# Projection in the order q, k, v, products moved from GpSimd to VectorE, and regrouped transposes in a one-core hybrid layer

## The chip, the cores and the metric

The kernel runs on one core of a Trainium2 chip. The core has a matrix engine (TensorE, PE in the profile; PEld are its weight loads), three engines for elementwise work (VectorE or DVE, ScalarE or ACT, GpSimd or POOL), and SyncE (SP), which issues most of the transfers that the 16 DMA engines carry out. The metric is the device time of one execution in microseconds (us), with smaller being better.

## The reference

One layer of an encoder on 512 tokens of width 1024, all in float32:

```python
h = rms_norm(x, norm1_g) * (1 + sc1) + sh1
z = h @ w_in
xr, xg, q, k, v, qi, ki, wi = jnp.split(z, ...)
y_rnn = rg_lru_branch(xr, xg, ...)
q = rms_norm(q.reshape(B, S, N_HEADS, HEAD_DIM), q_norm_g)
k = rms_norm(k.reshape(B, S, N_HEADS, HEAD_DIM), k_norm_g)
...
y_attn = dsa_attention(q, k, v, qi, ki, wi)
mix = jnp.concatenate([rms_norm(y_rnn, rg_out_g), rms_norm(y_attn, attn_out_g)], axis=-1) @ w_out
x = x + g1 * mix
h2 = rms_norm(x, norm2_g) * (1 + sc2) + sh2
ff = moe_ffn(h2.reshape(B * S, D), w_router, b_router, w1, b1, w2, b2).reshape(B, S, D)
return x + g2 * ff
```

The attention has 8 heads of 64; an indexer picks up to 128 keys for each query. In the last part every token goes to 4 of 32 experts; an expert multiplies its tokens by `w1` (1024 x 2048, 8 MB), applies a clamped gated unit, and multiplies by `w2` (1024 x 1024, 4 MB).

## The kernel before

The program is written in the order of the work, and a scheduler puts each engine's instructions in a fixed order: an instruction that is ready early by its estimate can pass others that stand before it in the source. Each engine then works through its own list, and waits where an operand isn't there.

**The head** (until about 400 us). The columns of z are made in pieces of 256 columns. `split_in` writes a piece of the weights as a rounded part (ScalarE, line 152) and a rest (line 153, on VectorE, or on GpSimd where the caller passes `G`, as for xr, xg and k); `mm3` (lines 157 to 159) adds three products of the parts. The order of the pieces is: v's second half with the indexer's keys, the indexer's queries, xr, xg, then k, v's first half, and q. `norm_heads` squares a head group on ScalarE (454), sums it on VectorE (455) and takes the inverse root in twelve small steps (`rstd_of`, lines 141 to 148). `prep_k` scales k on VectorE (462), transposes it on TensorE (468) and splits it (469, 470); `prep_q` does so for q (475 to 480) after a scaling of q's four tiles, which VectorE and GpSimd share (553). `rg_half` prepares the recurrent branch's half of the output product, and `split_out` the output weights: GpSimd multiplies them by the gate g1 (491), ScalarE and VectorE split them (492, 493). `rg_out_half` is one of eight products of that half; four stand before attention, four are given to `attend` as filling.

`attend` takes one tile of 128 queries through 8 heads: two products for the scores (576, 577), a masked minimum on VectorE (581), the exponential on ScalarE (582), transposes (587), a copy (588) and the products with the values (569). After the first `attend` the kernel splits the experts' first bias into three bf16 parts, on GpSimd (680 to 686). The output product's second half, the router and the norm of the second part follow.

**The experts** (from about 400 us to the end). SyncE loads all weights in order into 18 places of 1 MB (`wslot`, line 823): 8 for an expert's `w1`, 4 for its `w2`. A load waits until TensorE has read what lay in its place. The places lie in memory that the head uses until its end.

Experts are ranked by their number of tokens, and each rank has a number of 32-row blocks, `NBS`, 1 to 4 (86 in all). For expert j the loop issues: `gather` of expert j+2's rows from HBM (GpSimd, 855), `up(j)` (884), `glu(j)` (889 to 893), `turn_x(j+1)`, which transposes the gathered rows (863, copied by ScalarE and VectorE in turn, 864), `bias(j+1)` (870, 871), `down(j-1)` (911, 917), `add_out(j-1)`, which scales the result (930) and adds it to the output in HBM row by row (GpSimd, 933), and `turn_act(j)` (901, 902). `turn_x`, `bias`, `turn_act` and `route` take two PSUM banks in turn, 4 and 5; `up` writes banks 0 to 3, `down` banks 6 and 7. `up` and `down` use TensorE in tiles of 32 columns, the transposes use the whole array. `gather` and `add_out` move all of a rank's rows, 32 for each block, whether a slot holds a token or not. A loop at the end handles tokens beyond a rank's rows, in blocks of 128.

## Time and profile before

| | |
|---|---|
| median of 3 runs | 1457.71 us (1455.44 to 1466.08) |
| profiled execution | 1457.75 us |
| its span, first to last instruction | 1455.9 us |
| mean granted TensorE clock | 0.963 |
| busy: TensorE, VectorE, ScalarE, GpSimd | 1363.4, 547.6, 273.3, 204.1 us |
| DMA | 482.39 MB, mean 331 GB/s |

In the profile a line such as L491 is a line of the program. A row of a timeline gives start, duration, engine, line, operation, and in square brackets how long the engine had been idle and what released it. A row of the view by stretches gives each engine's busy time and instructions, the granted TensorE clock (1.00 is full speed), the mean busy share of the DMA engines, and GB/s. A row of the view by groups gives count, busy time, mean ns of one, idle time before, and its releasers.

### The profile page before, as it was taken

Reading aid. Unit: us, or ns where it says so; the run is one execution under the profiler, and the core shown is the slowest. Engines: PE = TensorE matmul, PEld = TensorE weight load, DVE = VectorE, ACT = ScalarE, POOL = GpSimd, SP = SyncE. Lnnn points to the kernel's source line nnn. Section 1 sums busy time; section 2 is a strip of 40 time slices with the busy share of each in tenths; the row PEclk is TensorE's granted clock in tenths of the full one; section 3 lists DMA queues with packets and bytes.
Section 4 is the critical chain, followed back from the end, with each engine's and each line's share of the span. In section 5 each row is a group of like instructions: output and inputs, shape, how many; then the busy total and the mean of one; then the engine's idle time right before and its main releaser. Section 6 shows DMA issues by size and latency. Waiting matters only on the chain. (4 is left out here: it accounts for less than half of the span.)

```text
span 1455.9 us, 26502 instructions
## 1 busy us (share of the span) xinstructions
PE 1363.4 (94%) x10907; PEld 611.4 (42%) x10907; DVE 547.6 (38%) x1317; ACT 273.3 (19%) x552; POOL 204.1 (14%) x238
## 2 busy tenths in 40 slices
PE   5999988999799999999999999999999999999993
PEld 2854887767533343334333333333333333333320
DVE  4579986755722222214212231223132122212221
ACT  4445553433111100101011000001010010100100
POOL 4312623511100010000001011000000000100000
PEclk9999999878689999999999999999999999999997
DMA  9676113014999999999999999999999999999995
GB/s 373 219 270 231 59 59 117 22 58 159 374 390 363 323 404 392 391 407 404 409 395 403 418 401 383 402 410 389 410 399 404 409 405 407 399 393 393 395 418 197
DMA packets 83398, 482.39 MB, mean 331 GB/s; under 512 B 11778, under 2 KB 14018, under 8 KB 33098
## 3 DMA queue, kind: packets, MB, share of 16 engines
q1 hardware_dynamic: 75034, 453.88, 77.8%
q0 software_dynamic: 7520, 24.68, 6.7%
q8 instruction: 87, 1.43, 0.4%
q10 hardware_dynamic: 720, 2.10, 0.4%
q14 instruction: 37, 0.30, 0.1%
HBM read 465.14 MB, written 15.48 MB: 330 GB/s over the span
## 5 line engine op out<-in xcount | busy, mean ns | idle before, releaser
L884 PE MATMUL bank<-mem,mem 128*32 128x512 f32 x5504 | 622.4, 595 | 0.0
L884 PEld LDWEIGHTS bank<-mem,mem 128*32 128x32 f32 x5504 | 174.6, 110 | 371.6 <-issue 363.2
L911 PE MATMUL bank<-mem,mem 128*32 128x512 f32 x2304 | 268.4, 593 | 0.0
L889 DVE TENSOR_TENSOR bank<-bank,mem 128x512 f32<-128x512 f32 x86 | 60.0, 697 | 410.1 <-PE bank L884 409.8
L911 PEld LDWEIGHTS bank<-mem,mem 128*32 128x32 f32 x2304 | 85.0, 110 | 146.0 <-issue 134.1
L891 ACT ACTIVATE mem<-bank 128x256 f32<-128x256 f32 x86 | 33.1, 385 | 527.8 <-DVE bank L889 527.8
L930 DVE SCALAR_TENSOR_TENSOR mem<-bank,gate_h,mem 64x512 f32<-64x512 f32 x72 | 54.0, 749 | 207.2 <-PE bank L911 206.5
L933 POOL DMA_INDIRECT out_dram<-mem,idx_all x32 | 47.0, 1470 | 581.7 <-DVE mem L930 525.9
L157 PE MATMUL bank<-mem,mem 128*128 128x512 f32 (+1 forms) x320 | 115.0, 362 | 2.9 <-DVE mem L522 2.3
L158 PE MATMUL bank<-mem,mem 128*128 128x512 f32 (+1 forms) x320 | 113.7, 355 | 0.0
L159 PE MATMUL bank<-mem,mem 128*128 128x512 f32 (+1 forms) x320 | 112.7, 352 | 0.0
L855 POOL DMA_INDIRECT mem<-h_d,idx_all x32 | 30.2, 943 | 400.4 <-PE bank L863 342.7
L157 PEld LDWEIGHTS bank<-mem,mem 128*128 128x128 f32 x320 | 62.3, 196 | 14.3 <-issue 3.5
L159 PEld LDWEIGHTS bank<-mem,mem 128*128 128x128 f32 x320 | 62.4, 195 | 12.9 <-issue 6.8
L917 PE MATMUL bank<-mem,mem 128*32 128x512 f32 x448 | 61.8, 601 | 6.0 <-SPq L1014 4.3
L158 PEld LDWEIGHTS bank<-mem,mem 128*128 128x128 f32 x320 | 62.6, 195 | 9.3 <-issue 3.5
L864 DVE COPY mem<-bank 128x512 f32<-128x512 f32 (+2 forms) x32 | 18.0, 564 | 112.5 <-PE bank L863 112.2
L863 PEld LDWEIGHTS bank<-ident,mem 128*128 128x128 f32 (+2 forms) x256 | 33.7, 196 | 58.7 <-issue 26.8
L902 ACT COPY mem<-bank 128x512 f32<-128x512 f32 (+1 forms) x32 | 18.3, 573 | 207.9 <-PE bank L911 115.3
L863 PE MATMUL bank<-ident,mem 128*128 128x128 f32 (+2 forms) x256 | 43.6, 295 | 11.2 <-ACT mem L902 5.1
L153 POOL TENSOR_TENSOR mem<-mem,mem 128x512 fp32r<-128x512 f32 (+1 forms) x28 | 41.2, 1490 | 86.4 <-ACT mem L152 86.3
L901 PEld LDWEIGHTS bank<-ident,mem 128*128 128x128 f32 x172 | 24.5, 207 | 37.5 <-issue 21.1
(325 smaller groups left out, 1216.9 us busy)
## 6 DMA issues: line engine op xcount, KB each, us to landing
mem<-in_w_dram SPq DMA_DIRECT2D x384, 1024.0 KB, 15.1
mem<-in_w_ada_dram SPq DMA_DIRECT2D x24, 1024.0 KB, 6.3
mem<-in_w_in_dram SPq DMA_DIRECT2D x20, 512.0 KB, 5.5
mem<-in_x_dram SPq DMA_DIRECT2D x8, 512.0 KB, 6.4
mem<-in_w_out_dram SPq DMA_DIRECT2D x8, 512.0 KB
mem<-in_w_in_dram SPq DMA_DIRECT2D x8, 256.0 KB, 5.9
mem<-mod_d SPq DMA_DIRECT2D x4, 512.0 KB, 6.0
h_d<-mem POOLq DMA_DIRECT2D x4, 512.0 KB, 8.6
```

The source lines that it names most:

```text
L153: (sub or V).tensor_sub(lo, src, hi)
L157: T.matmul(p, ah, bh, start=(k == 0), stop=False)
L158: T.matmul(p, al, bh, start=False, stop=False)
L159: T.matmul(p, ah, bl, start=False, stop=(k == n - 1))
L863: T.transpose(p[:, k, 0:n], xgs[frm][0:n, 4 * q + k::KD], ident[0:n, 0:n])
L884: T.matmul(bk[b][32 * n:32 * n + 32, :], xT[:, k, BT * b:BT * b + BT], w[k][:, 0, n * 512:(n + 1) * 512], start=(k == 0), stop=(k == KD - 1))
L889: V.tensor_add(bk[b], bk[b], biasb[j % 2])
L891: A.activation(act[:, b], u[:, :, 0], AF.Gelu_apprx_sigmoid)
L911: T.matmul(bk[6 + b // 2][o:o + 32, :], aT[:, b, c, BT * n:BT * n + BT], w[n][:, c, m * 512:(m + 1) * 512], start=(n + c == 0), stop=(n == ...
L917: T.matmul(bk[6 + nb // 2][o:o + 32, :], aT[:, nb - 1, c, BT * n:BT * n + BT], w[n][:, c, m * 512:(m + 1) * 512], start=(n == 0), stop=(n ...
L930: V.scalar_tensor_tensor(ys[64 * h:64 * h + a.stop - a.start, ns], p[a], gate_h[a, h, j:j + 1], g2h[a], op0=OP.mult, op1=OP.mult)
L933: G.indirect_dma_start(out=out_rows, out_offset=bass.IndirectOffsetOnAxis(ap=idx_all[a, j:j + 1], axis=0), in_=ys[a], in_offset=None, comp ...
```

## The change

- z's last pieces are made in the order q, k, v. q's load follows xr's weights, k's follows the rg inputs, v's comes last. q's norm, scaling and `prep_q` stand beside k's products; the weights of the recurrent half are split after k's second half, in the memory that k's weights leave; k's norm and `prep_k` stand beside and after v.
- The products with g1 in `split_out`, q's scaling and the bias split go from GpSimd to VectorE and ScalarE; the bias split is moved ahead of k's norm. The subtractions of line 153 for q and v go to GpSimd, where those for k are already.
- In the experts' loop `turn_x` stands after `down`, next to `turn_act`, and `add_out` after both. Its two copies are both on ScalarE. Where the current expert has fewer than four blocks, bank 3 is a third bank for `turn_x`, `bias` and `turn_act`.
- Each rank has a number of rows that is a multiple of 8 (2560 in all instead of 2752); `gather` and `add_out` move only those. The last 32 rows of the three gather buffers are cleared once.

```diff
     halves(ch_piece, w_xr, lambda a: (ev_xr, 2 * a), G)
-    w_k = load_in(R[0], 1536)
+    w_q = load_in(R[0], 1024)
     modulate(1)
     for b in range(4):
         rg_in(b)
+    w_k = load_in(R[1], 1536)
     halves(ch_piece, w_xg, lambda a: (ev_xg, 2 * a), G)
     rg_out()
-    w_v = load_in(R[1], 2048, 256)
+    w_v = load_in(R[2], 2048, 256)
...
-            G.tensor_mul(raw[b][:, 0], raw[b][:, 0], g1r)
+            V.tensor_mul(raw[b][:, 0], raw[b][:, 0], g1r)
...
-    halves(tok_piece, w_k, lambda a: (ev_tok(zk, 256 * a),), G)
-    rk = norm_heads(zk, "k", 191, rls)
-    tok_piece(w_v, ev_tok(zv, 0))
-    for pr in range(4):
-        prep_k(pr, rk)
-    w_q = load_in(R[2], 1024)
+    def split_b1():
+        for n in range(2):
...
+            V.tensor_scalar(b1o, b1o, 1.0, None, op0=OP.add)
+            A.copy(b1t[:, ns], b1f[0:96])
+            V.tensor_sub(b1f[0:96], b1f[0:96], b1t[:, ns])
+            for q in (1, 2):
+                c = slice(32 * q, 32 * q + 32)
+                A.copy(b1t[c, ns], b1f[c])
+            V.tensor_sub(b1f[64:96], b1f[64:96], b1t[64:96, ns])
+            A.copy(b1t[64:96, ns], b1f[64:96])
...
+    halves(tok_piece, w_q, lambda a: (ev_tok(zq, 256 * a),), G)
...
-    half_a = rg_half()
-    halves(tok_piece, w_q, lambda a: (ev_tok(zq, 256 * a),))
+    load_wo(0)
+    rq = norm_heads(zq, "q", 191.5, rls)
+    for i in range(NT):
+        z = zq[:, i].rearrange("p (h d) -> p h d", h=H)
+        V.tensor_mul(z, z, rq[:, i, :, None].to_broadcast([128, H, HD]))
+    k_half = lambda a: tok_piece(part_of(w_k, 256 * a, 256 * a + 256), ev_tok(zk, 256 * a), G)
+    k_half(0)
+    for pr in range(4):
+        prep_q(pr)
+    r_a = rg_half()
+    k_half(1)
+    half_a = (r_a, *split_out(0, R[1], grg))
+    split_b1()
+    rk = norm_heads(zk, "k", 191, rls)
+    tok_piece(w_v, ev_tok(zv, 0), G)
...
     load_wo(1)
+    for pr in range(4):
+        prep_k(pr, rk)
     rg = [partial(rg_out_half, i, n, *half_a) for i in (3, 2, 1, 0) for n in range(2)]
     for f in rg[0:4]:
         f()
-    rq = norm_heads(zq, "q", 191.5, [mem(174.75 + 2 * j, S) for j in range(2)])
-    for i in range(NT):
-        z = zq[:, i].rearrange("p (h d) -> p h d", h=H)
-        (G if i % 2 else V).tensor_mul(z, z, rq[:, i, :, None].to_broadcast([128, H, HD]))
-    for pr in range(4):
-        prep_q(pr)
...
+    ROWS = [96, 96, 128, 128, 128, 120, 112, 104] + [96] * 4 + [88] * 2 + [80] * 2 + [72] * 2 + [64] * 8 + [56] * 2 + [48] * 2 + [32] * 2
...
+    def spare(nb):
+        return bank(4, 5) if nb == 4 else bank(3, 4, 5)
...
-            (V.tensor_copy if q else A.copy)(xTs[j % 2][:, 4 * q:4 * q + 4, 0:n], p[:, :, 0:n])
+            A.copy(xTs[j % 2][:, 4 * q:4 * q + 4, 0:n], p[:, :, 0:n])
...
         if j + 1 < E:
-            turn_x(j + 1, xg_of(j + 1), NBS[j + 1])
-            bias(j + 1, bias_col(j + 1))
+            bias(j + 1, bias_col(j + 1), nb)
         if j:
             down(load_down(w2_of(expert(j - 1))), NBS[j - 1])
-            add_out(j - 1, NBS[j - 1])
+        if j + 1 < E:
+            turn_x(j + 1, xg_of(j + 1), NBS[j + 1], nb)
         if j < E:
             turn_act(nb)
+        if j:
+            add_out(j - 1, NBS[j - 1], ROWN[j - 1])
```

More of the change, by code (lines that the diff above doesn't have):

```diff
@@ L496, in layer @@
     ssA = const.tile([128, NT], F32)
-    mh, ml = mem(R[3] + 8, 4, S, dt=F32R), mem(R[4], 4, S, dt=F32R)
+    mh, ml = mem(R[3], 4, S, dt=F32R), mem(R[4], 4, S, dt=F32R)
     def rg_half():
@@ L512, in rg_half @@
             hilo(mh[:, b], ml[:, b], yR[:, b])
-        wh, wl = split_out(0, R[1], grg)
-        return r, wh, wl
+        return r
     def rg_out_half(i, n, r, wh, wl):
@@ L522, in rg_out_half @@
         V.scalar_tensor_tensor(part[:, i, ns], p, r[:, i:i + 1], part[:, i, ns], op0=OP.mult, op1=OP.add)
-    halves(tok_piece, w_k, lambda a: (ev_tok(zk, 256 * a),), G)
-    rk = norm_heads(zk, "k", 191, rls)
-    tok_piece(w_v, ev_tok(zv, 0))
-    for pr in range(4):
-        prep_k(pr, rk)
-    w_q = load_in(R[2], 1024)
+    b1t = const.tile([96, 2 * FF], BF)
+    def split_b1():
+        for n in range(2):
+            ns = slice(n * FF, (n + 1) * FF)
+            b1f = mem(161.75, FF)
+            for j in range(3):
+                nc.sync.dma_start(b1f[32 * j:32 * j + 32], b1[0, :, ns])
+            b1o = b1f[0:96].rearrange("p (f two) -> p f two", two=2)[:, :, 1]
+            V.tensor_scalar(b1o, b1o, 1.0, None, op0=OP.add)
[6 more added lines that the diff above has]
+            A.copy(b1t[64:96, ns], b1f[64:96])
     wo_v = w_out[0].rearrange("(b p) n -> p b n", p=128)
@@ L614, in mix_in @@
         r = rstd_of(ssB, 512, "rB")
-        bh, bl = [mem(R[3] + 2 * j, 4, 128, dt=F32R) for j in range(2)]
+        bh, bl = [mem(R[3] + 8 + 2 * j, 4, 128, dt=F32R) for j in range(2)]
         p = bank(4, 5).rearrange("p (b t) -> p b t", b=4)
@@ L671, in layer @@
     half_b = split_out(1, R[5], gat)
-    b1t = const.tile([96, 2 * FF], BF)
-    for n in range(2):
-        ns = slice(n * FF, (n + 1) * FF)
-        b1f = mem(R[3] + 4, FF)
-        for j in range(3):
-            nc.sync.dma_start(b1f[32 * j:32 * j + 32], b1[0, :, ns])
-        b1o = b1f[0:96].rearrange("p (f two) -> p f two", two=2)[:, :, 1]
-        G.tensor_scalar(b1o, b1o, 1.0, None, op0=OP.add)
-        G.tensor_copy(b1t[:, ns], b1f[0:96])
-        for j in range(1, 3):
-            for q in range(j, 3):
-                c = slice(32 * q, 32 * q + 32)
-                G.tensor_sub(b1f[c], b1f[c], b1t[c, ns])
-                G.tensor_copy(b1t[c, ns], b1f[c])
     m3 = mix_in(3)
@@ L713, in layer @@
     NBS = [BLOCKS[r] for r in ORDER]
+    ROWN = [ROWS[r] for r in ORDER]
     xgs = [mem(144, D), mem(112, D), mem(116, D)]
@@ L851, in route, with gather, turn_x, bias @@
         V.tensor_copy(gate_h[:, :, e0:e0 + n], p[:, 0:16].rearrange("p (r e) -> p r e", r=2)[:, :, 0:n])
-    def gather(r, to, nb):
-        a = slice(0, BT * nb)
+    def gather(r, to, rows):
+        a = slice(0, rows)
         G.indirect_dma_start(out=xgs[to][a], out_offset=None, in_=h2_d,
                              in_offset=bass.IndirectOffsetOnAxis(ap=idx_all[a, r:r + 1], axis=0))
-    def turn_x(j, frm, nb):
+    def spare(nb):
+        return bank(4, 5) if nb == 4 else bank(3, 4, 5)
+    def turn_x(j, frm, nb, of=4):
         n = BT * (4 if nb == 3 else nb)
         for q in range(2):
-            p = bank(4, 5).rearrange("p (k t) -> p k t", k=4)
+            p = spare(of).rearrange("p (k t) -> p k t", k=4)
             for k in range(4):
                 T.transpose(p[:, k, 0:n], xgs[frm][0:n, 4 * q + k::KD], ident[0:n, 0:n])
-            (V.tensor_copy if q else A.copy)(xTs[j % 2][:, 4 * q:4 * q + 4, 0:n], p[:, :, 0:n])
-    def bias(j, col):
-        p = bank(4, 5)
+            A.copy(xTs[j % 2][:, 4 * q:4 * q + 4, 0:n], p[:, :, 0:n])
+    def bias(j, col, of=4):
+        p = spare(of)
         for n in range(4):
@@ L964, in layer @@
     xg_of = lambda j: 2 - j if j < 2 else (j - 2) % 3
+    for t in xgs:
+        G.memset(t[96:128], 0.0)
     places(selb, gts, 0, 2)
     route(0, 2)
-    gather(0, xg_of(0), NBS[0])
-    gather(1, xg_of(1), NBS[1])
+    gather(0, xg_of(0), ROWN[0])
+    gather(1, xg_of(1), ROWN[1])
     rank_experts()
@@ L978, in layer @@
         if j + 2 < E:
-            gather(j + 2, xg_of(j + 2), NBS[j + 2])
+            gather(j + 2, xg_of(j + 2), ROWN[j + 2])
         if j < E:
@@ L1052, in layer @@
         route(0, 1, lambda i, e: posE[:, i:i + 1], lambda i, e: payE[:, i, :])
-        gather(0, 0, 4)
+        gather(0, 0, CAP)
         turn_x(0, 0, 4)
```

11 lines of the change are left out of this document (5 added, 6 removed).

## The prediction

> **What bounds the kernel now.** I read the page first, then busy time by stretch, then the engines' timelines at each place where TensorE stopped.
>
> The page says that TensorE and the DMA engines are both full from about 400 us on. A coarse cut shows which one sets the end:
>
> ```profile
> q1 hardware_dynamic: 75034, 453.88, 77.8%
> q0 software_dynamic: 7520, 24.68, 6.7%
> ```
>
> ```profile
> core 0: us, PE busy (x) PEld busy (x) DVE busy (x) ACT busy (x) POOL busy (x), PEclk, DMA share, GB/s
> ...
> 358.40:402.00 43.60, 34.24 (x227) 24.82 (x227) 33.52 (x151) 10.66 (x32) 6.76 (x9) 0.69 0.96 363
> 402.00:425.00 23.00, 23.00 (x178) 6.61 (x177) 1.31 (x11) 1.87 (x2) 0.98 (x1) 0.84 1.01 419
> 425.00:505.00 80.00, 79.39 (x714) 29.91 (x710) 23.73 (x63) 9.17 (x20) 5.23 (x5) 1.00 0.92 340
> 505.00:1425.00 920.00, 893.57 (x8000) 307.97 (x7996) 234.04 (x523) 88.02 (x185) 66.31 (x54) 1.00 1.01 401
> 1425.00:1438.00 13.00, 7.24 (x60) 1.31 (x52) 1.50 (x2) 0.37 (x1) 1.42 (x1) 0.95 0.93 369
> ```
>
> From 505 to 1425 us the DMA share is 1.01: the queues never run dry for 920 us, while TensorE leaves 26 us of it. The end agrees: the last down product is held up by its weights.
>
> ```profile
> 1434.49 1.07 PE L917 MATMUL bank<-mem,mem 128*32 128x512 f32 x8 [1.38 <-SPq L1014]
> 1438.23 1.93 PE L917 MATMUL bank<-mem,mem 128*32 128x512 f32 x8 [2.67 <-SPq L1014]
> ```
>
> So the expert stage ends when the weight stream ends, and its length is bytes over rate. A faster TensorE buys only what it frees before 505 us, where the share is 0.92 and loads wait for a slot to be read. What else moves the end is the time at which the stage begins, that is the head. There the same view shows three stretches in which TensorE idles, and then runs at a low granted clock:
>
> ```profile
> 164.00:199.00 35.00, 34.74 (x288) 34.33 (x287) 29.28 (x45) 17.34 (x31) 21.86 (x13) 1.00 0.26 97
> 199.00:201.00 2.00, 0.03 (x1) 0.04 (x1) 1.76 (x9) 0.80 (x2) 0.00 (x0) 1.00 0.00 0
> 201.00:206.70 5.70, 4.33 (x20) 3.63 (x20) 5.67 (x14) 3.45 (x4) 0.00 (x0) 0.70 0.01 3
> 206.70:248.20 41.50, 40.96 (x268) 34.65 (x268) 28.96 (x53) 18.28 (x30) 4.76 (x2) 1.00 0.27 102
> 248.20:254.70 6.50, 1.81 (x9) 1.01 (x9) 5.53 (x7) 2.08 (x3) 6.10 (x4) 0.82 0.01 3
> 254.70:262.60 7.90, 7.65 (x16) 4.54 (x16) 6.85 (x11) 3.76 (x6) 1.48 (x1) 0.50 0.00 0
> ...
> 291.60:297.70 6.10, 2.61 (x8) 1.69 (x7) 6.01 (x12) 1.42 (x4) 5.33 (x5) 0.64 0.00 0
> 297.70:310.40 12.70, 12.67 (x40) 9.98 (x41) 2.44 (x6) 1.89 (x5) 0.00 (x0) 0.50 0.01 1
> ```
>
> Idle time plus busy time times the missing clock gives each loss. A, 199 to 206.7: 1.97 + 1.37 idle, 4.33 x 0.30 = 1.3 of clock, 4.6 us. B, 248.2 to 262.6: 4.7 + 0.25 idle, 0.3 + 3.8 of clock, 9.1 us. C, 291.6 to 310.4: 3.5 idle, 0.9 + 6.3 of clock, 10.7 us. Together 24.4 us. The timelines name one cause for all three, VectorE's small instructions beside GpSimd's large ones. First VectorE, then GpSimd, then TensorE:
>
> ```profile
> 191.61 2.32 DVE L143 TENSOR_SCALAR mem<-mem 128x32 int32<-128x32 int32 x1
> ...
> 198.68 0.19 DVE L147 TENSOR_TENSOR mem<-mem 128x32 f32<-128x32 f32 x1
> ...
> 241.74 2.33 DVE L143 TENSOR_SCALAR mem<-mem 128x32 int32<-128x32 int32 x1
> 244.10 0.18 DVE L144 TENSOR_SCALAR mem<-mem 128x32 int32<-128x32 int32 x1
> ...
> 289.72 1.98 DVE L146 SCALAR_TENSOR_TENSOR rB<-rB 128x1 f32<-128x1 f32 x1
> ...
> 292.72 0.54 DVE L581 CUSTOM_DVE_ANT_0 mem<-bank,mem 128x384 f32<-128x384 f32 x1
> ```
>
> ```profile
> 189.14 9.46 POOL L491 TENSOR_TENSOR mem<-mem,mem 128x1024 f32<-128x1024 f32 x4 [12.74 <-DMA mem<-in_w_out_dram]
> 239.28 4.76 POOL L491 TENSOR_TENSOR mem<-mem,mem 128x1024 f32<-128x1024 f32 x2 [40.67 <-DMA mem<-in_w_out_dram]
> 248.60 2.94 POOL L553 TENSOR_TENSOR mem<-mem,mem 128x512 f32<-128x512 f32 x2 [4.57 <-issue]
> ...
> 287.34 4.35 POOL L685 TENSOR_TENSOR mem<-mem,b1t 32x1024 f32<-32x1024 f32 x2
> ```
>
> ```profile
> 200.97 2.33 PE L468 MATMUL bank<-ident,mem 128*128 128x128 f32 x8 [1.98 <-DVE mem L462]
> ...
> 254.64 0.80 PE L157 MATMUL bank<-mem,mem 128*128 128x512 f32 x1 [2.28 <-DVE mem L522]
> ...
> 257.39 0.79 PE L576 MATMUL bank<-mem,mem 128*128 128x512 f32 x1 [0.25 <-DVE mem L480]
> ...
> 294.06 0.90 PE L587 MATMUL bank<-ident,mem 128*128 128x128 f32 x3 [2.46 <-ACT mem L582]
> ```
>
> A norm step of 0.19 us takes 2.3 us while a product of L491 runs, one step for each product. k's norm ends late (A), q's norm and the two GpSimd tiles of L553 end late (B), and in attention the norm steps behind L685 delay the score reduction L581, on which the exponentials and so the transposes wait (C).
>
> **The change, part by part.** Costs of the instructions that move:
>
> ```profile
> L153 POOL TENSOR_TENSOR mem<-mem,mem 128x512 fp32r<-128x512 f32 x24 | 34.3, 1447 | 82.8 <-ACT mem L152 82.7
> ...
> L153 DVE TENSOR_TENSOR mem<-mem,mem 128x512 fp32r<-128x512 f32 x16 | 10.2, 682 | 0.2 <-ACT mem L152 0.2
> L493 DVE SCALAR_TENSOR_TENSOR mem<-mem,svt,mem 128x1024 fp32r<-128x1024 f32 x7 | 8.9, 1281 | 0.1
> L470 DVE SCALAR_TENSOR_TENSOR mem<-bank,svt,mem 64x512 fp32r<-64x512 f32 x8 | 6.0, 749 | 0.2
> L462 DVE TENSOR_TENSOR mem<-mem,mem 128x256 f32<-128x256 f32 x16 | 5.7, 418 | 0.1
> ```
>
> *Order q, k, v.* Today q's norm, its scaling and its transposes stand between the last product of z and the first score. They move beside k's products; what now stands there is k's norm and prep_k, beside v's 96 matmuls (288 in 34.74 us, so 11.6 us), the 48 of the recurrent half and 32 transposes (268 in 40.96 us, so 12.2 us): 23.8 us of cover. On VectorE it is one reduction and twelve norm steps (about 3 us), 16 x 0.418, 8 x 0.749 and four L493 for the output weights, which now wait until k leaves their place: 3 + 6.7 + 6.0 + 5.1 = 20.8 us. It fits by 3 us, so I take most of B back but not all, since the margin is thin: 4 of 9.1. The loads keep their number; q takes k's load time, k v's, and w_out follows q as it followed k, so the SP queue brings nothing later to a product. Bounds: 0 and 9.1.
>
> *Products off GpSimd.* A's cause goes: L491 leaves, and k's norm now has only v's subtractions near it: 4 of 4.6. C's cause goes: the bias split L680 to L686 leaves attention; 7 of 10.7, because a reduction delayed by VectorE's own new work can leave a gap there. VectorE gains 8 products at two 128x512 of 0.682 (10.9 us), two scalings of one 128x512 (1.4 us), and six instructions of the bias split, between 0.68 and 1.36 each: 4 to 8 us. It gives the 12 subtractions for q and v, of 0.682 (8.2 us), to GpSimd: 8 to 12 us more in all. VectorE has 12.5 us free between 206.7 and 248.2, but four of the products stand beside attention, where its reductions are waited for, so I charge 3 us (about half of those four); bounds 0 and 12. ScalarE's eight copies for the bias lie in its 23 us of idle in that stretch. Head: 4 + 4 + 7 - 3 = 12 us earlier.
>
> The GpSimd rows show an exclusive hold: a step ends when the product ends. The Trainium skill, SBUF — State Buffer, section Who interferes with whom, has a rule that speaks against the change: a GpSimd instruction that reads SBUF and a VectorE instruction with two SBUF inputs shut each other out entirely. By that rule the 12 subtractions that go to GpSimd would take back up to what they last; the rows of L143 and L146 agree with it.
>
> *Rows.* The 32 experts gather and scatter 2560 rows instead of 2752, each way. q0's share is 6.7% of 1455.9, 97.5 us for 24.68 MB, so 2 x 192 rows of 4 KB (1.57 MB) are 6.2 us of a stream that is never idle after 505 us, where nearly all of them lie. The three clearings of xgs lie on GpSimd before the first gather, which waits for the routing.
>
> *Transposes and banks.* Rows and act are transposed together, and small experts rotate three banks. TensorE's short waits between products go or shrink:
>
> ```profile
> 735.61 0.71 PE L863 MATMUL bank<-ident,mem 128*128 128x128 f32 x4 [0.76 <-ACT mem L902]
> ...
> 739.07 0.60 PE L863 MATMUL bank<-ident,mem 128*128 128x128 f32 x3 [0.68 <-ACT mem L871]
> ```
>
> Two such waits are 1.4 us; at 1 us per expert it is 30 us of TensorE's time, and nearly nothing of the end: the stream bounds it. The scatter's products L930 now queue on VectorE behind the copy of act; only the next down product waits for their banks, a whole up stage later. Only the idle share before 505 us counts, 0.08 x 80 = 6.4 us, of which three experts' earlier releases return 2. Both copies of the rows on ScalarE cost the first expert one 0.6 us copy, the one place without cover. Expert stage: 6.2 + 2 - 1 = 7 us; bounds 0 and 12.
>
> Sum, against the profiled execution's 1457.75 us (span 1455.9; the median of the runs is 1457.71): 1457.75 - 12 - 7 = 1439 us.
>
> **The rivals.**
> *The stalls only move.* New gaps of the reordered engines call the low clock as often; for it, each of the three gaps of some 2 us above was followed by a lower clock (0.70, 0.50, 0.50), so a single one in attention costs what C did. Against it, all three have the one cause that leaves. The head stays: 1457.75 - 7 = 1451.
> *VectorE becomes the end of the head* (slower). If the scheduler puts all new VectorE work, 10.9 + 8 us, ahead of k's norm, and the eight subtractions for k's second half and v on GpSimd (8 x 1.447 = 11.6 us) hold it as L491 did, 20.8 grows to 51 us against 23.8 of cover: 27 us idle in place of B's 5, A's 4.6 back, C as lost as now: +18. It decides once VectorE's work after k exceeds the cover by 17 us (B's 5, A's 4.6 and the expert stage's 7). 1457.75 + 18 - 7 = 1468. Against it: the products with g1r and the bias need nothing of k and VectorE has gaps earlier.
> *The rows save nothing.* Row numbers such as 88 or 104 aren't multiples of 16; if the busiest DMA engine carries 8 rows for 120, 104 and 88, 6 for 72 and 4 for 56, the packets at 97.5 x 16 / 6025 = 0.26 us on it fall by one row each way in all, 0.5 us: 1457.75 - 12 - 1.3 = 1444. The Trainium skill, DMA: Bandwidth & Descriptors, section Why a DMA increments its semaphore by 16 and not by 1, states such a rule (engines used: the largest divisor up to 16); every count so far is a multiple of 32, so no run here shows it.
> *An expert exceeds its rows.* Then the loop at the end runs once: 12.6 MB at 401 GB/s is 31 us, none of it hidden, so about 1490. By the reference's routing of its inputs the closest changed slot has 72 rows for 70 tokens, so this is unlikely.
>
> **How the numbers follow.** Forecast 0.60, own range 1428 to 1448 (C or B return wholly, or neither); stalls move 0.20; rows save nothing 0.09; VectorE 0.08; overflow 0.03. The range 1424 to 1460 leaves out the last two and the forecast's far ends. Over 1% faster, about what a measurement tells, is below 1443: three quarters of the forecast and half of the rows' rival, 0.49. Slower by over 1%, above 1472: the overflow and a tail of VectorE's, 0.05. The rest, 0.46, is no change.
>
> **What would show it.** Norm steps at 0.2 us throughout 164 to 310; the first score matmul near 250 instead of 257.4; no 0.50 clock about 300; a full DMA share from about 493 us on, not 505, and to the end; q0 near 6.3%. Wrong: a TensorE gap before the first score that VectorE releases, or idle DMA late in the expert stage.

## The result: about as forecast in all, with other parts than forecast

| | before | after |
|---|---|---|
| median of 4 runs each | 1457.51 us | 1440.72 us (1440.13 to 1441.37) |
| profiled execution, its span | 1457.75, 1455.9 us | 1441.37, 1439.6 us |
| mean granted TensorE clock | 0.963 | 0.968 |
| first score product | 257.4 us | 259.5 us |
| first load of expert weights issued | 321.8 us | 311.0 us |
| first up product | 402.0 us | 390.1 us |
| first up product to the end | 1053.9 us | 1049.5 us |

The ratio is 0.988, with a 95% interval of 0.986 to 0.990. The forecast of 1439 us lies 2 us from the median. The head is 11.9 us shorter (12 were forecast) and the expert stage 4.4 us (7 were forecast). That looks like a forecast that worked; the stretches say otherwise. The first score comes no earlier (259.5 us against 257.4), where 7 us earlier was expected. These times are of one execution: in the seven kernels of this study that share this head line for line, the first score came at 256.8 to 259.5 us and the first load at 308.2 to 311.1, so differences of that size say nothing. This is the profile after, by stretches (columns as before: each engine's busy time, granted clock, DMA share, GB/s):

```profile
core 0: us, PE busy (x) PEld busy (x) DVE busy (x) ACT busy (x) POOL busy (x), PEclk, DMA share, GB/s
164.00:199.00 35.00, 28.14 (x214) 27.54 (x213) 27.11 (x38) 24.18 (x36) 22.46 (x16) 0.90 0.24 80
...
206.80:213.00 6.20, 2.05 (x16) 1.65 (x14) 6.10 (x6) 2.13 (x4) 5.42 (x4) 0.92 0.00 1
213.00:226.00 13.00, 12.38 (x79) 9.59 (x79) 8.69 (x18) 6.62 (x11) 0.00 (x0) 0.77 0.00 1
226.00:259.50 33.50, 32.88 (x225) 29.28 (x225) 29.96 (x62) 18.34 (x29) 0.00 (x0) 1.00 0.27 95
259.50:348.50 89.00, 88.83 (x467) 69.72 (x465) 50.27 (x178) 35.91 (x95) 4.49 (x5) 0.90 0.19 71
...
440.00:493.00 53.00, 53.00 (x494) 17.26 (x486) 15.16 (x30) 6.37 (x14) 2.42 (x2) 1.00 0.97 362
493.00:1409.00 916.00, 896.53 (x7988) 300.64 (x7992) 219.31 (x494) 100.46 (x215) 68.08 (x55) 1.00 1.01 401
```

In attention (259.5 to 348.5 us) TensorE now hardly waits (88.83 us busy of 89), where C stood before: from the first score product to the last product with the values it is 91.7 us, and was 104.0. The clock in that row is still 0.90: from 324.7 to 341.8 us it is 0.50 with no hole ahead of it that the profile shows (24.70 us busy in the 24.7 us before), as it was from 337.7 to 351.3 us in the old kernel. The prediction counted low clock behind holes only. Ahead of attention there are two new holes, in rows that were full before: 28.14 busy in 35 us, and 2.05 in 6.2 us, with a clock of 0.77 behind it. TensorE's timeline names their ends:

```profile
173.27 0.58 PE L157 MATMUL bank<-mem,mem 128*128 128x256 f32 x1 [6.11 <-ACT mem L306]
...
211.17 0.33 PE L476 MATMUL bank<-ident,mem 128*128 128x128 f32 x1 [2.81 <-DVE mem L560]
212.84 1.89 PE L476 MATMUL bank<-ident,mem 128*128 128x128 f32 x4 [1.34 <-DVE mem L560]
```

The first hole ends with a copy of ScalarE, line 306, which empties the last bank of xg. ScalarE's and VectorE's timelines show why it came late (line 539 is a copy of the moved bias split, 536 its subtraction, 403 the four scans of the recurrent branch):

```profile
169.85 1.04 ACT L539 CAST b1t<-mem 32x1024 bf16<-32x1024 f32 x1 [7.63 <-DVE mem L536]
170.92 0.62 ACT L152 CAST mem<-mem 128x512 fp32r<-128x512 f32 x1
171.56 1.04 ACT L539 CAST b1t<-mem 32x1024 bf16<-32x1024 f32 x1
172.63 0.59 ACT L306 COPY mem<-bank 128x512 f32<-128x512 f32 x1
```

```profile
158.88 8.80 DVE L403 TENSOR_TENSOR_SCAN mem<-mem,mem 128x512 f32<-128x512 f32 x4 [0.51 <-POOL mem L402]
167.60 2.21 DVE L536 TENSOR_TENSOR mem<-mem,b1t 96x1024 f32<-96x1024 f32 x1
```

The bias split stands in the source behind k's second half, but all its operands are ready early, so the scheduler puts its first half at 156 to 178 us. Its copy waits 7.6 us on ScalarE for a subtraction that stands on VectorE behind 8.8 us of scans, and an evacuation that needs nothing of either waits in the same list behind it.

The second hole ends with q's scaling, line 560. VectorE first, then GpSimd:

```profile
206.70 0.19 DVE L146 SCALAR_TENSOR_TENSOR mem<-mem 128x32 f32<-128x32 f32 x1
206.93 1.24 DVE L147 TENSOR_TENSOR mem<-mem 128x32 f32<-128x32 f32 x1
208.20 1.19 DVE L148 SCALAR_TENSOR_TENSOR mem<-mem 128x32 f32<-128x32 f32 x1
209.43 3.96 DVE L560 TENSOR_TENSOR mem<-mem,mem 128x512 f32<-128x512 f32 x3
```

```profile
206.82 5.42 POOL L153 TENSOR_TENSOR mem<-mem,mem 128x512 fp32r<-128x512 f32 x4 [5.16 <-ACT mem L152]
```

A norm step goes from 0.19 to 1.2 us at the instant at which GpSimd starts on v's subtractions, which the change gave to it. This is the old fault with smaller instructions.

The end of the expert stage and its software queue (packets, MB, share) read:

```profile
1418.29 1.06 PE L932 MATMUL bank<-mem,mem 128*32 128x512 f32 x8 [1.39 <-SPq L1033]
1421.91 1.94 PE L932 MATMUL bank<-mem,mem 128*32 128x512 f32 x8 [2.56 <-SPq L1033]
```

```profile
q0 software_dynamic: 7488, 23.11, 6.4%
```

The weights still end last, and the queue's share fell to 6.4% as forecast (6.3%). For what the rows saved, the time at which each load lands says more. In the table every load is timed from the issue of the first one, as the trace's transfers have it (the loads are counted from 0, so the 80th is the 81st to land):

```
kernel             first load   80th landed   last landed   80th to last
before                 321.8        +280.7       +1115.7          835.0
after                  311.0        +274.5       +1110.3          835.8
```

All that the stage gained was gained by the 80th load, at about 585 us. Over the remaining 300 loads, where most of the rows move, nothing was gained.

### The profile page after: what moved, and what is told of

It reads as the page before. It is cut to its first block, busy times and chain, and to the rows that moved or that the text cites. A ratio compares the mean times of both kernels' runs of the same rounds, so it can differ in the third digit from the quotient of the medians.

```text
span 1439.6 us, 26492 instructions
## 1 busy us (share of the span) xinstructions
PE 1356.1 (94%) x10907; PEld 596.1 (41%) x10907; DVE 526.7 (37%) x1289; ACT 294.5 (20%) x592; POOL 179.5 (12%) x227
## 5 line engine op out<-in xcount | busy, mean ns | idle before, releaser
L899 PE MATMUL bank<-mem,mem 128*32 128x512 f32 x5504 | 624.1, 594 | 0.0
L899 PEld LDWEIGHTS bank<-mem,mem 128*32 128x32 f32 x5504 | 175.8, 110 | 371.3 <-issue 359.1
L926 PE MATMUL bank<-mem,mem 128*32 128x512 f32 x2304 | 273.9, 596 | 0.1
L926 PEld LDWEIGHTS bank<-mem,mem 128*32 128x32 f32 x2304 | 76.8, 110 | 157.9 <-issue 146.0
L932 PE MATMUL bank<-mem,mem 128*32 128x512 f32 x448 | 68.9, 601 | 5.9 <-SPq L1033 4.2
L153 POOL TENSOR_TENSOR mem<-mem,mem 128x512 fp32r<-128x512 f32 (+1 forms) x40 | 59.8, 1513 | 103.3 <-ACT mem L152 103.2
L879 ACT COPY mem<-bank 128x512 f32<-128x512 f32 (+2 forms) x64 | 30.5, 487 | 175.5 <-PE bank L878 126.8
L916 PE MATMUL bank<-ident,mem 128*128 128x128 f32 x172 | 32.7, 308 | 7.6 <-DVE mem L908 7.5
```

Source lines behind the costliest of these rows:

```text
L153: (sub or V).tensor_sub(lo, src, hi)
L899: T.matmul(bk[b][32 * n:32 * n + 32, :], xT[:, k, BT * b:BT * b + BT], w[k][:, 0, n * 512:(n + 1) * 512], start=(k == 0), stop=(k == KD - 1))
L926: T.matmul(bk[6 + b // 2][o:o + 32, :], aT[:, b, c, BT * n:BT * n + BT], w[n][:, c, m * 512:(m + 1) * 512], start=(n + c == 0), stop=(n == ...
L932: T.matmul(bk[6 + nb // 2][o:o + 32, :], aT[:, nb - 1, c, BT * n:BT * n + BT], w[n][:, c, m * 512:(m + 1) * 512], start=(n == 0), stop=(n ...
```

## The experiments

Three questions were left: what made the head shorter, what the rows and the loop each gave, and whether the two holes could be closed. Ratios are to the kernel before, with their 95% intervals.

**Whole blocks of rows again.**

```diff
-    ROWN = [ROWS[r] for r in ORDER]
+    ROWN = [BT * n for n in NBS]
```

> The changed kernel, with every rank moving 32 rows for each block again (2752 rows each way instead of 2560). Theory 1, the mean load counts: the gathers and scatters take 90.5 us of each DMA engine for 5120 rows in the changed kernel, 0.0177 us per row, so 384 more rows lengthen the time from the first load of expert weights to the last landing (1110 us in the changed kernel, 1116 before) by 6 to 7 us, to 1447 us in all. Theory 2, the busiest engine counts: by the counting of the prediction's rival (8 rows on the busiest engine for 120, 104 and 88, 6 for 72, 4 for 56) it carries 171 rows each way in the changed kernel and 172 with whole blocks, so nothing moves beyond 0.5 us: 1441 us. Between the 80th and the 384th load the landings of the two known traces stay 16 to 17 us apart, which speaks for theory 2.

1440.09 us (1438.4 to 1440.8), ratio 0.987 (0.985 to 0.989); the last load landed 1110.3 us after the first was issued, to the tenth as in the changed kernel, although q0 moved 24.68 MB again:

```profile
q0 software_dynamic: 7520, 24.68, 6.8%
```

So the 6 to 7 us of theory 1 aren't there: the smaller row counts of the change were worth nothing that these runs can tell.

**Rows at multiples of 16.**

```diff
-    ROWS = [96, 96, 128, 128, 128, 120, 112, 104] + [96] * 4 + [88] * 2 + [80] * 2 + [72] * 2 + [64] * 8 + [56] * 2 + [48] * 2 + [32] * 2
+    ROWS = [96, 96, 128, 128, 128, 128, 112, 112] + [96] * 6 + [80] * 4 + [64] * 10 + [48] * 2 + [32] * 2
```

> The changed kernel, with every rank's rows raised to the next multiple of 16 (120 to 128, 104 to 112, 88 to 96, 72 to 80, 56 to 64; 2624 rows each way instead of 2560). Theory 1, the mean load counts: 128 more rows at 0.0177 us are 2.3 us later, 1443 us. Theory 2, the busiest engine counts: it carries 164 rows each way instead of 171, and a row takes about 0.33 us to scatter and 0.20 us to gather in the trace, so 7 x 0.53 = 3.7 us earlier, 1437 us, although more bytes move. The two signs differ; the length from first weight load to last landing (1110.3 us in the changed kernel) should show it to a few tenths.

1435.9 us (1434.8 to 1442.1), ratio 0.985 (0.983 to 0.988), last landing at +1106.3. The sign and the size are those of theory 2. But the interval overlaps that of the run before it, and the time from first issue to last landing varies from one execution to another: four kernels with the changed loop and the changed rows, the changed kernel among them, gave 1108.8 to 1115.1. By itself this run is not proof, which is why the row count was taken to extremes below.

**The old order in the experts' loop.**

```diff
-        return bank(4, 5) if nb == 4 else bank(3, 4, 5)
+        return bank(4, 5)
...
-            A.copy(xTs[j % 2][:, 4 * q:4 * q + 4, 0:n], p[:, :, 0:n])
+            (V.tensor_copy if q else A.copy)(xTs[j % 2][:, 4 * q:4 * q + 4, 0:n], p[:, :, 0:n])
...
-            bias(j + 1, bias_col(j + 1), nb)
+            turn_x(j + 1, xg_of(j + 1), NBS[j + 1])
+            bias(j + 1, bias_col(j + 1))
         if j:
             down(load_down(w2_of(expert(j - 1))), NBS[j - 1])
-        if j + 1 < E:
-            turn_x(j + 1, xg_of(j + 1), NBS[j + 1], nb)
+            add_out(j - 1, NBS[j - 1], ROWN[j - 1])
         if j < E:
             turn_act(nb)
-        if j:
-            add_out(j - 1, NBS[j - 1], ROWN[j - 1])
```

> The changed kernel, with the experts' loop in its old order: transposes of rows before the down products with copies on both engines, two banks in turn for all, the scaling and scatter before the transposes of act. The rows stay at 2560. In the changed kernel the weights gain 6 us on the old kernel between the first load (10.8 us earlier) and the 80th (17.0 us earlier), and nothing after it. Theory A: the gain comes from TensorE, which frees places earlier while the loads still wait for them; then the old order gives back 3 to 6 us, 1444 to 1447 us, and the DMA share in the first 100 us of the expert stage falls from 0.98 to 0.93 or so. Theory B: the gain is that the stage starts earlier against loads that are fixed by something else (the first rows, the routing); then 0 to 1 us, 1441 us.

1444.11 us (1442.7 to 1448.4), ratio 0.990 (0.988 to 0.993). The 80th load landed at +279.7 and the last at +1115.9, as before the change (+280.7, +1115.7). The stretches at the beginning of the stage, of this kernel and then of the changed one:

```profile
389.00:412.00 23.00, 23.00 (x182) 6.66 (x181) 1.26 (x10) 1.87 (x2) 0.98 (x1) 0.85 1.01 419
412.00:439.00 27.00, 26.38 (x234) 9.02 (x226) 8.52 (x33) 2.80 (x6) 1.83 (x2) 1.00 0.91 349
439.00:492.00 53.00, 53.00 (x488) 21.01 (x484) 15.22 (x30) 6.36 (x14) 3.36 (x3) 1.00 0.93 337
```

```profile
390.00:413.00 23.00, 23.00 (x198) 6.90 (x197) 3.72 (x23) 2.35 (x3) 0.99 (x1) 0.94 1.01 416
413.00:440.00 27.00, 26.23 (x222) 8.85 (x218) 8.02 (x32) 2.71 (x6) 1.84 (x2) 1.00 0.97 368
440.00:493.00 53.00, 53.00 (x494) 17.26 (x486) 15.16 (x30) 6.37 (x14) 2.42 (x2) 1.00 0.97 362
```

Theory A holds: TensorE is full in both, but in these 103 us it gets through 914 products in the changed loop (198 + 222 + 494) and 904 in the old one (182 + 234 + 488), places come free earlier, and the DMA share is 0.97 instead of 0.91 and 0.93. The granted clock of the first stretch differs too, 0.94 against 0.85, but it isn't what counts: in the eight kernels with the changed loop and at most 2752 rows each way, whose clock at that point varied as well, the 80th load landed at +273.4 to +275.5, and in the three with the old loop at +279.7 to +280.9. As far as the runs show, the whole of the shorter expert stage comes from this.

**The bias split put back behind the first attend, still on VectorE and ScalarE.**

```diff
-            b1f = mem(161.75, FF)
+            b1f = mem(R[3] + 12, FF)
...
-    split_b1()
     rk = norm_heads(zk, "k", 191, rls)
...
     half_b = split_out(1, R[5], gat)
+    split_b1()
```

> The changed kernel, with the split of the experts' first bias put back after the first attend (same instructions on VectorE and ScalarE, in memory that k leaves free, so that it cannot run earlier). Theory A: in the changed kernel the split runs at 156 to 174 us, where ScalarE's copies wait 7.6 us behind a subtraction of VectorE that stands behind four scans; the evacuation of xg's last bank waits behind them, TensorE stands for 6.1 us and then has a low clock for 6.8 us. Without the split there the gap goes: 6 us idle and up to 3 us of clock, 1432 to 1435 us. Theory B (rival): the scans and their products with GpSimd are what holds that stretch, so another wait takes the gap's place, or the split's steps delay the score reductions in attention as in the old kernel (its loss C was 10.7 us): between 1438 and 1450 us, with TensorE gaps in the attends released by VectorE or ScalarE.

1434.27 us (1430.7 to 1438.9), ratio 0.984 (0.981 to 0.987). The first load of weights comes at 302.5 us instead of 311.0. The 6.1 us hole is gone, and attention takes 92.1 us against 91.7, with no gap of TensorE over 0.6 us in it: theory A. In the norm behind the first attend the steps take 0.15 us, and the split's subtractions 1.2 us beside them.

**The old kernel with nothing but the products taken off GpSimd.**

```diff
-            G.tensor_mul(raw[b][:, 0], raw[b][:, 0], g1r)
+            V.tensor_mul(raw[b][:, 0], raw[b][:, 0], g1r)
...
-        (G if i % 2 else V).tensor_mul(z, z, rq[:, i, :, None].to_broadcast([128, H, HD]))
+        V.tensor_mul(z, z, rq[:, i, :, None].to_broadcast([128, H, HD]))
...
-        G.tensor_copy(b1t[:, ns], b1f[0:96])
+        A.copy(b1t[:, ns], b1f[0:96])
...
-                G.tensor_sub(b1f[c], b1f[c], b1t[c, ns])
+        V.tensor_sub(b1f[0:96], b1f[0:96], b1t[:, ns])
```

> The old kernel, with the one part changed that takes GpSimd's products out of the head: the products with g1 and the scaling of q all on VectorE, the bias split on VectorE and ScalarE at its old place after the first attend. The order of z, the experts' loop and the rows stay old. Theory 1, the prediction's cause: the three losses A (4.6 us, at 199 us), B (9.1 us, at 248 us) and C (10.7 us, at 292 us) come from VectorE's steps standing beside GpSimd's products; A and C then go wholly and B in half, the first load of expert weights comes at 303 to 307 us instead of 321.8 and the time is 1439 to 1444 us. Theory 2, the rival: the eight products that now stand on VectorE, at 1.3 us each and in k's and q's norm, take back what they free; the first load comes at 312 to 320 us and the time is 1448 to 1456 us. In both the expert stage keeps its 1054 us.

1437.29 us (1435.4 to 1440.4), ratio 0.987 (0.984 to 0.990): at least as fast as the whole change, with the old order of z, the old loop and the old rows. In VectorE's timeline the steps of k's norm are at 0.19 us where they took up to 2.3; the second fence is the row of the weight loads (count, ns of one issue, first and last start in us):

```profile
192.79 0.19 DVE L148 SCALAR_TENSOR_TENSOR mem<-mem 128x32 f32<-128x32 f32 x1
193.01 0.19 DVE L146 SCALAR_TENSOR_TENSOR mem<-mem 128x32 f32<-128x32 f32 x1
193.24 0.19 DVE L147 TENSOR_TENSOR mem<-mem 128x32 f32<-128x32 f32 x1
```

```profile
L824 SPq DMA_DIRECT2D mem<-in_w_dram x384: 327/333/580, 298.5 to 1395.8; - x192
```

298.5 us against 321.8 is 23.3 us, almost the whole of A, B and C (24.4). It divides as they do: the first score comes at 244.9 us, 12.5 earlier (A and B are 13.7), and attention takes 93.8 us instead of 104.0 (C is 10.7). All three had the one cause that the prediction named, B as well: with the products away, q's norm and scaling are quick enough in their old place. In B it also held an instruction that the prediction didn't name, a product of line 669 in the old kernel, which stood ahead of the evacuation on which TensorE waited for 2.28 us. It took 2.35 us there, beside a product of L491, and takes 0.23 us here:

```profile
251.57 2.35 DVE L669 TENSOR_TENSOR mem<-onesb,later 128x128 bf16<-128x128 bf16 x1 [0.93 <-POOL mem L553]
```

**The changed order with the products given back to GpSimd.**

```diff
-            V.tensor_mul(raw[b][:, 0], raw[b][:, 0], g1r)
+            G.tensor_mul(raw[b][:, 0], raw[b][:, 0], g1r)
...
-        V.tensor_mul(z, z, rq[:, i, :, None].to_broadcast([128, H, HD]))
+        (G if i % 2 else V).tensor_mul(z, z, rq[:, i, :, None].to_broadcast([128, H, HD]))
...
-            b1f = mem(161.75, FF)
+            b1f = mem(R[3] + 12, FF)
...
-            A.copy(b1t[:, ns], b1f[0:96])
+            G.tensor_copy(b1t[:, ns], b1f[0:96])
...
-    split_b1()
     rk = norm_heads(zk, "k", 191, rls)
...
     half_b = split_out(1, R[5], gat)
+    split_b1()
```

> The changed kernel, with the products given back to GpSimd (those with g1, half of q's scaling, and the bias split at its old place after the first attend). The order q, k, v, the loop and the rows stay as changed. Theory 1: the products are the cause of the losses, the order only moves them; q's norm now stands beside the first products with g1, the bias split delays the reductions in attention as it did, and the first load of expert weights comes at 315 to 322 us (321.8 in the old kernel, 311.0 in the changed one, 302.5 with the bias split put back on VectorE and ScalarE): 1445 to 1452 us. Theory 2: the order alone hides B (9.1 us) behind k's products; the first load comes at 310 to 313 us and the time is 1439 to 1443 us.

1439.11 us (1437.0 to 1442.5), ratio 0.987 (0.984 to 0.990); first load at 308.2 us. By the numbers that is 2 us better than theory 2 had it, and far from theory 1. q's norm does meet three products with g1, as theory 1 said, but k's products stand beside it and TensorE waits for only 1.8 us:

```profile
200.15 2.32 DVE L146 SCALAR_TENSOR_TENSOR mem<-mem 128x32 f32<-128x32 f32 x1
```

And C is gone although GpSimd makes the bias split in attention, since the split ends 0.7 us before the norm steps behind the first attend begin (GpSimd, then VectorE):

```profile
281.69 1.03 POOL L540 CAST b1t<-mem 32x1024 bf16<-32x1024 f32 x1
```

```profile
283.37 0.15 DVE L141 TENSOR_SCALAR rB<-ssB 128x1 f32<-128x1 f32 x1 [0.33 <-ACT mem L634]
```

In the old kernel the split ran from 268.7 to 297.2 us and the norm from 286.1 us on. Here it lies in memory that k leaves, and so starts at 253.3 us. C was an overlap of two things in time, not a price of the split. In exchange there is a new hole of 6.55 us at 171 us, where squares on ScalarE wait 8.35 us for a product of GpSimd that stands behind two products with g1, and a bank's copy waits behind them. So theory 2 met the time by another way than its own. The first load is 13.6 us earlier than in the old kernel, but the first score only 1.0 us (256.4 against 257.4): the order hid A and B and brought holes of nearly the same price. The other 12.6 us are in attention (91.4 us instead of 104.0), and there, by the timelines, it was the earlier place of the bias split that took C away, not the hiding of B behind k's products.

**v's subtractions on VectorE** (on top of the bias split behind the first attend).

```diff
-    tok_piece(w_v, ev_tok(zv, 0), G)
+    tok_piece(w_v, ev_tok(zv, 0))
```

> The changed kernel with the bias split put back after the first attend, and the four subtractions of v's weights on VectorE, behind the scaling of q, instead of on GpSimd. Theory A: in that kernel two norm steps of q and the four scalings take 1.2, 1.2 and 4.6 us while GpSimd makes v's subtractions, and TensorE stands for 2.8 and 1.3 us with 6.8 us of low clock behind it; alone the steps take 0.2 us and the scalings 0.7 us each, so 4 us of idle and 2 to 3 us of clock go: the first load of weights comes 5 to 7 us earlier (at 296 to 298 us instead of 302.5) and the time is 1428 us against 1434. Theory B: the products with g1 that stand between the norm steps (1.2 to 2.2 us each) are the larger part and v's subtractions lengthen VectorE's list before k's norm by 2.7 us: the first load within 2 us of 302.5, 1433 to 1436 us.

1427.54 us (1425.1 to 1431.3), ratio 0.980 (0.977 to 0.983); first load at 299.1 us, first score at 246.3 us. The first load alone says little: the next kernel has the same head and 295.5 us. But the hole is theory A's: the scalings of q take 2.50 us for four, the two waits before line 476 (2.81 and 1.34 us) are gone, and the clock from 200 us to the first score is 1.00 instead of 0.93. The products with g1, which are still between the norm steps, cost no gap.

```profile
199.96 0.19 DVE L146 SCALAR_TENSOR_TENSOR mem<-mem 128x32 f32<-128x32 f32 x1
200.19 0.19 DVE L147 TENSOR_TENSOR mem<-mem 128x32 f32<-128x32 f32 x1
200.41 0.19 DVE L148 SCALAR_TENSOR_TENSOR mem<-mem 128x32 f32<-128x32 f32 x1
200.64 2.50 DVE L560 TENSOR_TENSOR mem<-mem,mem 128x512 f32<-128x512 f32 x4
```

**The same with the rows at multiples of 16.** The edit is the one to `ROWS` above.

> The same as the kernel before it in this list, with the ranks' rows at multiples of 16. If the busiest engine sets the stream, as the run with these rows alone showed (1106.3 us from first load to last landing instead of 1110.3), this is again 4 us less, 1424 to 1426 us if theory A holds there, 1430 if theory B does; if that difference was chance, it is equal to it.

1425.31 us (1420.7 to 1426.5), ratio 0.977 (0.975 to 0.980). It is the fastest kernel of the study, by the medians 15 us below the changed kernel and 32 below the old one. But the 2 us against the kernel above lie within the intervals, and in the profiled executions they came from the head, which is the same program (first load at 295.5 us), and not from the loads (last landing +1111.1 against +1109.3). The 4 us that rows at multiples of 16 seemed to give weren't seen again.

**One row count for all experts.** Three kernels differ from the changed one only in how many rows each gather and each scatter moves. They are for timing alone, since rows past an expert's blocks carry leftovers into the output:

```diff
     def gather(r, to, rows):
-        a = slice(0, rows)
+        a = slice(0, 104)
...
-        a = slice(0, rows)
+        a = slice(0, 104)
         G.indirect_dma_start(out=out_rows, out_offset=bass.IndirectOffsetOnAxis(ap=idx_all[a, j:j + 1], axis=0),
```

> The changed kernel, with every expert's gather and scatter moving 104 rows whatever its rank (3328 rows each way instead of 2560); the computing stays, rows beyond an expert's blocks carry what lies there and rows of a larger expert beyond 104 are left out. This measures the cost of a row count by itself. Theory 1, the mean load counts: 1536 more rows at 0.0177 us are 27 us, 1468 us. Theory 2, the busiest engine counts, with 8 rows on it for 104: 32 x 8 = 256 rows each way instead of 171, 85 x 0.53 = 45 us, 1486 us.

> The same with 112 rows for every expert (3584 rows each way). Theory 1: 36 us more than the changed kernel, 1477 us, 9 us more than with 104. Theory 2: 7 rows on the busiest engine, 224 rows each way, 53 x 0.53 = 28 us more than the changed kernel, 1469 us, so 17 us less than with 104 although more bytes move.

> The same with 128 rows for every expert (4096 rows each way). Theory 1: 54 us more than the changed kernel, 1495 us, 27 us more than with 104. Theory 2: 8 rows on the busiest engine as with 104, the same time as with 104, 1486 us.

104 rows: 1481.62 us (1478.5 to 1483.0). 112 rows: 1467.93 us (1466.6 to 1473.8). 128 rows: 1458.21 us (1455.1 to 1462.1). The time *falls* as the rows grow. In theory 1 it had to rise (1468, 1477, 1495). Theory 2 met the first two (1486, 1469) and missed the third by 28 us: by its counting 128 rows load the busiest engine as 104 do, but they cost 23 us less. So both fall as they stood. The queues' rows of the three, in that order:

```profile
q0 software_dynamic: 10208, 29.41, 8.3%
```

```profile
q0 software_dynamic: 9184, 31.50, 8.6%
```

```profile
q0 software_dynamic: 10208, 35.69, 9.2%
```

The own time of the rows' packets rises with the bytes, 8.3 to 9.2%, as theory 1 has it. What falls must be elsewhere, and it is in the weights. For this table the packets of the trace between 420 and 1400 us were sorted: row packets (4 KB) under 320 ns are the gathers', the others the scatters'; a weight packet (8 KB) counts as beside a gather if it starts within 0.15 us of the start of one of its rows.

```
                      gather row   weight packet beside a gather    beside a scatter   beside neither
kernel                  mean ns       mean ns    over 400 ns            mean ns            mean ns
before                    192           388          44%                  322                315
after                     200           403          53%                  323                314
whole blocks again        194           391          46%                  323                313
multiples of 16           191           389          43%                  325                313
104 for all               217           432          71%                  320                312
112 for all               199           395          51%                  323                314
128 for all               159           314           1%                  322                312
```

Beside scatters a weight packet takes the same in all seven kernels. Beside gathers it takes 25 to 40% longer, except where all gathers have 128 rows, and then it takes no longer at all. That holds for each gather by itself, within one execution. In the old kernel, these are the gathers after 415 us with no scatter between issue and landing (weight packets beside them sorted as above):

```
rows of the gather   gathers   gather row, ns   weight packet beside it, ns   over 400 ns
64                         6        212                   419                     55%
96                         6        222                   433                     61%
128                        2        159                   309                      0%
```

Against 309 ns, the usual length, the lengthening beside gathers sums to 31.5 us per engine with 104 rows, 18.9 with 112 and 1.2 with 128; in the changed kernel it is 15.9, with whole blocks 13.9. Added to the row packets' own time per engine (120.7, 125.4 and 133.0 us with 104, 112 and 128 rows, 90.5 in the changed kernel) that is 152, 144 and 134 us against 106: 46, 38 and 28 us more than the changed kernel, where the times rose by 41, 27 and 17. The order is that of the times; the sizes are 5 to 11 us too large. Between the old rows and the changed ones the packets' own time fell by 5.6 us (96.1 to 90.5) and 2 to 3 us of it come back beside the gathers (13.9 or 13.1 to 15.9). The change took three of the six ranks with 128 rows to 120, 112 and 104; at 0.6 to 1.0 us for a gather (18.9 and 31.5 us for 32 of them) that would be 2 to 3 us, an estimate. The 3 us left over are within what the stream varies by.

Why a gather of fewer than 128 rows lengthens the weights' packets is not settled. It isn't whether 16 divides the count: it does for 64, 96 and 112. A kernel that gathers 128 rows always and scatters only a rank's rows would be the test, and perhaps a gain of some 5 us: 4096 x 0.159 less 2560 x 0.200 us over 16 engines cost 9 us more, the weights give 14.7 back. It wasn't tried.

**The old order with everything else.** The order k, v, q, the products off GpSimd, the bias split behind the first attend, and the changed loop, with rows at multiples of 16:

```diff
-    halves(tok_piece, w_q, lambda a: (ev_tok(zq, 256 * a),), G)
+    halves(tok_piece, w_k, lambda a: (ev_tok(zk, 256 * a),), G)
...
+    halves(tok_piece, w_q, lambda a: (ev_tok(zq, 256 * a),))
```

> The order of z as in the old kernel (k, v, q), with the products off GpSimd and the bias split after the first attend, and with the changed kernel's loop and rows, these at multiples of 16. Theory 1, the order is worth nothing once the products are away: the first load of weights at 297 to 300 us (298.5 in the old kernel with the products moved, 295.5 to 299.1 in the new order with v's subtractions on VectorE), the loop's 5.5 us and up to 4 us for the rows: 1428 to 1431 us, against 1425.3 us in the new order. Theory 2, the order hides 4 us as the prediction had it: 1430 us or more, with the first load 4 us later than 295.5 to 299.1 and gaps before the first score.

1426.81 us (1424.5 to 1433.8), ratio 0.980 (0.978 to 0.983), against 1425.31 us in the new order (0.975 to 0.980): no difference that these runs can tell, though the intervals don't exclude the 4 us of theory 2. Its profiled execution, the second slowest of its five (1432.86 us), has the first load at 304.7 us, later than theory 1 said and as theory 2 had it. That doesn't decide either: its head is line for line that of the old kernel with the products moved, which had 298.5, so two executions of one head lie 6 us apart. The two kernels compared differ in one thing more, q's eight subtractions, which are on VectorE here. By the time theory 1 is met; that the order is worth nothing is not shown, only that it is worth too little for these runs.

## Why the prediction was right, and where it was not

The total was right and 2 us off. Its terms were not, and they cancelled, which is luck: the products gave 23 us and the loop 5.5, the two new holes took 12, and the rows gave nothing, which leaves 16.5 of the 16.8 us measured.

- **What bounds the expert stage**: right. The share from 493 to 1409 us is 1.01 (it was to be full from 493 on), the last down product still waits for weights, and whatever shortens the head shortens the whole nearly one for one (first load 302.5 us and 1434 us, 299.1 and 1428, against 311.0 and 1441).
- **The cause of A, B and C**: right, and worth more than was put into the sum. Products off GpSimd alone brought the first load 23.3 us earlier. One of the rows that the prediction set beside the rule on two SBUF inputs doesn't bear on it: L143 reads one tile. It was held for 2.3 us all the same; the steps with two tiles begin at L146.
- **Order q, k, v, "4 of 9.1"**: not borne out. The sign for it, the first score near 250, came at 259.5 us. B leaves with GpSimd's scaling and products alone (first score at 244.9 us in the old order); the order on top of that adds nothing that the runs can tell (1425.3 against 1426.8 us). The 23.8 us of cover for k's norm was there, and k's norm ran at 0.19 us per step; but the prediction followed k's norm alone and never asked what stands beside q's norm in its new place.
- **C, "7 of 10.7"**: went wholly. From the first score to the last values it was 104.0 us and is 91.7. That "a reduction delayed by VectorE's own new work can leave a gap" was not seen. The cause as stated, the split on GpSimd, was incomplete: with the split still there, but 15 us earlier, C is gone too.
- **VectorE's new work, "3 us, in attention"**: a charge was due, but in another place, by another way and of another size. The bias split cost 8.5 us (first load 311.0 against 302.5), ahead of attention, through ScalarE's list and not VectorE's load. The prediction said its copies "lie in its 23 us of idle"; the sum of the idle time was right, but one copy with a late operand holds everything behind it. And the prediction took the split to stand where the source has it, though it had said that the scheduler lets early work pass.
- **The twelve subtractions on GpSimd**: the rule cited against the change spoke truly. Four of them, 5.4 us long, cost 4.15 us of waits and a stretch at half clock behind them; by the medians it is 7 us (1434.3 to 1427.5), in intervals that overlap (0.981 to 0.987 and 0.977 to 0.983). The rule is the exclusive hold of the Trainium skill, SBUF — State Buffer, section Who interferes with whom; the step of 1.24 us (0.19 alone), and its return to 0.19 when the subtractions leave, agree with it. It was named and then not put into the sum.
- **Rows, 6.2 us**: wrong, nothing seen. The share of q0 fell nearly as forecast and the end didn't move (1440.7 us with them, 1440.1 without). The step that failed is the reading of "a stream that is never idle" as bytes at a fixed price: a gather of fewer than 128 rows also lengthens the weights' packets beside it (395 to 433 ns for 64 to 112 rows, against 309), and the change made three more of them.
- **Rival "the rows save nothing"** (0.09): its outcome came, its mechanism only in part. The Trainium skill, DMA: Bandwidth & Descriptors, section Why a DMA increments its semaphore by 16 and not by 1, has the engines used as the largest divisor up to 16. The runs with 104 and 112 rows came within 5 us of a time worked out by it, and the run with 128 rows came 28 us below, so the busiest engine is not what sets the stream. Within one kernel, too, gathers of 64, 96 and 128 rows, all of which have 16 as that divisor, differ (419, 433 and 309 ns for the weights beside them).
- **The loop, "2 us" of early idle share**: mis-sized. It measured 5.2 to 5.6 us (last landing +1115.9 against +1110.3, and 80th +279.7 against +274.5). The share rose from 0.91 to 0.97 over 27 us and from 0.93 to 0.97 over 53 us, which is 3.7 us of it and more than the third of 6.4 us that the prediction let return; where the rest was gained the runs don't say.
- **Rival "the stalls only move"** (0.20): half true. Two new holes, each with a stretch of 6.8 us at half clock (171.1 to 177.9, 212.1 to 218.9 us), took 12 us (first load 311.0 against 299.1) of the 23 that the products gave.

## What to carry to other kernels

Taking GpSimd's large two-input products away from the time of VectorE's small steps was worth as much alone as the whole change; look for such pairs first, and check every new neighbour of a moved step, not only the one that was late. An instruction with a late operand on an in-order engine is dear however idle that engine is: pin work that is ready too early behind something, for instance by the memory that it uses. A stream at full DMA share isn't shortened by each byte left out; time the loads from the first issue to the n-th landing, and vary the row count itself before rows are trimmed. One profiled execution places the end of such a head to some 3 to 6 us; a hole in it, and what ends the hole, is the surer sign.

## What was not expected of the hardware

- A gather of 128 rows cost the weights' stream less than one of 64, 96, 104 or 112, in one execution and between kernels. With one count for all: packets of 159 ns against 217 and 199 for the rows, and 314 against 432 and 395 ns for the weights beside them. With all gathers and scatters at 128 rows the kernel moves 60% more rows than the changed one (4096 for 2560 each way) and takes 1458 us instead of 1441; with 104 it takes 1482.
- The time from first issue to last landing of one and the same loop and rows differed by up to 6 us between kernels with different heads (1108.8 to 1115.1 us), more than some of the effects looked for; the time to the 80th landing was steady to 1.5 us (274.1 to 275.4).
